# Stick-breaking heads of two pairs begun together: products adjacent, masks after them, the second set inside the next V projection

## The chip, the cores and the metric

The kernel runs on one core of a Trainium2 chip. The metric is the device time of one execution in microseconds (us). The time before is the median of three runs; beside them stands one profiled execution, from which all rows here come.

## What is computed

A decoder trunk of two layers on 256 tokens of width 1024 in float32. Layer 0 runs 8 stick-breaking heads and 4 differential heads on one input projection, then an output projection and an MLP; layer 1 is a sparse attention with its own MLP. The change touches the stick-breaking heads of layer 0 alone:

```python
def stick_breaking_attention(q, k, v):
    ...
        z = jnp.einsum("bqhd,bkhd->bhqk", qb, k).astype(jnp.float32) * scale
        log_beta = jax.nn.log_sigmoid(z)
        log_rem = jnp.where(past, jax.nn.log_sigmoid(-z), 0.0)
        tail = lax.cumsum(log_rem, axis=3, reverse=True) - log_rem
        w = jnp.where(past, jnp.exp(log_beta + tail), 0.0)
        return jnp.einsum("bhqk,bkhd->bqhd", w.astype(v.dtype), v)
```

The heads are 64 wide, and `past` is strict: a query sees only earlier keys.

## The kernel before

Activations stay in SBUF, in two token tiles of 128 and transposed in eight slices of 128 features. Each weight arrives by DMA in two halves (`Weights.load`, L48), is split into a high part by ScalarE (`wh`, L66) and a low part by VectorE (`wl`, L69), and is kept in four rotating buffers; `get` (L78) splits one weight ahead in the program's order. A projection is three products per slice: high by high, high by low, low by high. A product of float32 operands (scores, values) appears as two records in the trace.

The work is written with a tile framework. Python order gives each instruction its priority; the framework then orders every engine's queue, and it may place an instruction that is ready ahead of an earlier one that is not. It also puts in all waits. Each engine works its queue in the order so made.

Layer 0's mixer (`even_mixer`, L487) goes in this order: V of the stick-breaking heads (`project_v`, L492: 24 products of 512 columns for token tile 0 into one PSUM bank, a copy by ScalarE, then 24 for tile 1 into another); the first halves of Q and K (`halves`, L511: `ps_f` products, copied to `qsb` and `ksb` by ScalarE at L509); the first set, `sb_start` for pairs 0 and 1 (L520); the second halves of Q and K; `sb_weights` for pairs 0 and 1; the second set, `sb_start` for pairs 2 and 3 (L523); `scalars` (L163: five small loads, one tiny product `ps_lam` and a few small operations for lambda); V of the differential heads, `project_v("dfv")`; `sb_values` of pairs 0 and 1 (`osb`); `sb_weights` of pairs 2 and 3; then the differential heads' projections and scores (`sdf`).

A pair is two heads, which lie on the lower and upper 64 partitions of `q` and `k`. `sb_start` (L552) takes a score tile `z` of two PSUM banks, one for each head. There are two such tiles, so pairs 2 and 3 use those of pairs 0 and 1 again. For each head it issues two products on 64 rows (256 columns, then 128) and two masks, products of the 128 x 128 identity with the mask in bfloat16 on all 128 rows. Then comes the softplus of the pair: three steps on ScalarE (`sb_e`, L569 to L571: absolute value, exponential, logarithm), and on VectorE `sb_sp` (L572), its high part `sb_h` (L573) and its low part `sb_l` (L574). `sb_weights` (L577) adds the suffix sums to `z` by products on `sb_h`, then `sb_l`, and ScalarE writes `sb_w` as the exponential (L586), the last reader of `z`.

Of the kernel before, what the change touches and what calls it, by code (L numbers as in the profile page):

```python
# [10 lines left out]
F32 = mybir.dt.float32  # L11
# [7 lines left out]
P = 128  # L19
S = 256  # L20
# [65 lines left out]
class Trunk:  # L86
# [400 lines left out]
    def even_mixer(self, xT, oT, pool, out):  # L487
        nc = self.nc
        vsb = pool.tile([P, 2, 512], F32, name="vsb")
        vdf = pool.tile([P, 2, 512], F32, name="vdf")  # L490

        def project_v(key, dst):  # L492
            w = [self.W.get((key, 0)), None]
            pss = [self.bankB("ps_v0"), self.bankB("ps_v1")]
            self.tmajor(pss[0], w[0], xT, 0, range(4), True, False)
            w[1] = self.W.get((key, 1))
            self.tmajor(pss[0], w[1], xT, 0, range(4, 8), False, True)
            nc.scalar.copy(dst[:, 0, :], pss[0])
            self.run_late()
            self.tmajor(pss[1], w[0], xT, 1, range(4), True, False)  # L500
            self.tmajor(pss[1], w[1], xT, 1, range(4, 8), False, True)
            nc.scalar.copy(dst[:, 1, :], pss[1])

        def project_f(key, i, dst, scale):
            w = self.W.get((key, i))
            for m in range(2):
                ps = self.bankB("ps_f")
                self.fmajor(ps[:, :S], w, m, xT)
                nc.scalar.activation(dst[:, 2 * i + m, :], ps[:, :S], AF.Copy, scale=scale)  # L509

        def halves(i, a, b, q, k):  # L511
            project_f(a, i, q, 0.125)
            project_f(b, i, k, 1.0)

        qsb = pool.tile([P, 4, S], F32, tag="q", name="qsb")
        ksb = pool.tile([P, 4, S], F32, tag="k", name="ksb")
        project_v("sbv", vsb)
        halves(0, "sbq", "sbk", qsb, ksb)
        with self.tc.tile_pool(name="ps_sb", bufs=2, space=PSUM) as banks:
            sb = {pr: self.sb_start(pr, qsb, ksb, pool, banks) for pr in (0, 1)}  # L520
            halves(1, "sbq", "sbk", qsb, ksb)
            w = {pr: self.sb_weights(sb[pr], pool) for pr in (0, 1)}
            sb = {pr: self.sb_start(pr, qsb, ksb, pool, banks) for pr in (2, 3)}  # L523
            self.scalars()
            project_v("dfv", vdf)
            for pr in (0, 1):
                self.sb_values(pr, w[pr], vsb, oT)
            w = {pr: self.sb_weights(sb[pr], pool) for pr in (2, 3)}
        qdf = pool.tile([P, 4, S], F32, tag="q", name="qdf")
        kdf = pool.tile([P, 4, S], F32, tag="k", name="kdf")  # L530
        halves(0, "dfq", "dfk", qdf, kdf)
        for pr in (2, 3):
            self.sb_values(pr, w[pr], vsb, oT)
        with self.tc.tile_pool(name="ps_df", bufs=4, space=PSUM) as banks:
            a = {h: self.df_weights(h, qdf, kdf, pool, banks) for h in (0, 1)}
            halves(1, "dfq", "dfk", qdf, kdf)
            o = {h: self.df_values(h, a[h], vdf, pool) for h in (0, 1)}
            a = {h: self.df_weights(h, qdf, kdf, pool, banks) for h in (2, 3)}
            for h in (0, 1):
                self.df_norm(h, o[h], oT, pool)  # L540

            def rest0():
                for h in (2, 3):
                    o[h] = self.df_values(h, a[h], vdf, pool)

            def rest1():
                for h in (2, 3):
                    self.df_norm(h, o[h], oT, pool)

            return out(banks, (rest0, rest1))  # L550

    def sb_start(self, pr, q, k, pool, banks):  # L552


        nc = self.nc
        z = banks.tile([P, 1024], F32, tag="z", name=f"z{pr}").rearrange("p (h c) -> p h c", h=2)
        N = S + P
        for h in range(2):
            d = slice(64 * h, 64 * h + 64)
            self.mm(z[:, h, :S], k[d, pr, :P], q[d, pr, :], True, False, skip_group_check=True)  # L560
            self.mm(z[:, h, S:N], k[d, pr, P:], q[d, pr, P:], False, False, skip_group_check=True)
            for c in (0, S):
                self.mm(z[:, h, c : c + P], self.identb, self.maskb, False, False, skip_group_check=True)
        zv = z[:, :, :N]
        e = pool.tile([P, 2, N], F32, tag="sb_e", name="sb_e", bufs=2)
        sp = pool.tile([P, 2, N], F32, tag="sb_sp", name="sb_sp", bufs=2)
        sph = pool.tile([P, 2, N], F32R, tag="sb_h", name="sb_h", bufs=2)
        spl = pool.tile([P, 2, N], F32R, tag="sb_l", name="sb_l", bufs=2)
        nc.scalar.activation(e, zv, AF.Abs)  # L569
        nc.scalar.activation(e, e, AF.Exp, scale=-1.0)  # L570
        nc.scalar.activation(e, e, AF.Ln, bias=1.0)  # L571
        nc.vector.scalar_tensor_tensor(sp, zv, 0.0, e, op0=ALU.max, op1=ALU.add)  # L572
        nc.vector.tensor_copy(sph, sp)  # L573
        nc.vector.tensor_sub(spl, sp, sph.bitcast(F32))  # L574
        return z, sph, spl
# [584 lines left out]
```

## Time and profile before

| what | value |
|---|---|
| median of three runs | 667.12 us |
| lowest run | 666.63 us |
| the profiled execution | 669.41 us |
| its span, first to last instruction | 667.7 us |
| mean granted TensorE clock | 0.985 |

The profile's engines are PE (TensorE's products), PEld (its weight loads), DVE (VectorE), ACT (ScalarE), POOL (GpSimd) and SP, which issues the loads. A record has its start from the beginning of the span and its length; records of products overlap, as the engine is pipelined. "Idle before" is the time for which the engine had stood, with the instruction that ended it. The granted clock is the share of 2.4 GHz that TensorE had.

### The profile page before, as it was taken

To read this page: it belongs to the slowest core of one execution; us is meant where nothing else is said; L and a number is where in the kernel's file an instruction comes from. 1 tells how busy PE (TensorE), PEld (TensorE's weight loads), DVE (VectorE), ACT (ScalarE), POOL (GpSimd) and SP (SyncE) were. 2 spreads that over 40 slices of the span, in tenths; PEclk is the share of its full clock that TensorE was granted. 3 is DMA by queue.
4 is the path that set the end of the run, shared out by engine and by line. 5 is a ranking of instruction groups with operands and counts; after the bars stand their busy time and mean duration, and the time that the engine had idled before them with its cause. 6 is when DMAs were issued, how large, how long until landed. Compare 5 with 4: busy or idle time off the path is not lost.

```text
span 667.7 us, 11136 instructions
## 1 busy us (share of the span) xinstructions
PE 647.5 (97%) x4257; PEld 566.6 (85%) x4257; DVE 408.4 (61%) x820; ACT 346.7 (52%) x699; POOL 46.3 (7%) x139
## 2 busy tenths in 40 slices
PE   6899999999999999999999989999999999999995
PEld 3798898889989898988898878777899899998984
DVE  5854637886555555555877485776775555555534
ACT  5565556555444444444567464753554445454423
POOL 3200000000000000000203321430000000000000
PEclk7999899999999999999999999999999999999998
DMA  7784243346555555555597632023365555656601
GB/s 255 229 261 138 71 149 127 116 156 212 188 183 189 182 182 183 184 186 143 155 319 243 194 110 64 1 64 124 110 222 180 188 188 190 189 190 185 192 2 63
DMA packets 74277, 108.67 MB, mean 163 GB/s; under 512 B 5072, under 2 KB 60400, under 8 KB 74224
## 3 DMA queue, kind: packets, MB, share of 16 engines
q1 hardware_dynamic: 74224, 107.97, 50.6%
q8 instruction: 33, 0.54, 0.3%
q14 instruction: 20, 0.16, 0.1%
HBM read 106.91 MB, written 1.05 MB: 162 GB/s over the span
## 4 chain that ended last, share of the span: by engine, by line
PE 90%; DVE 5%; ACT 2%; issue 1%; DMA 1%; SPq 0%; ACTq 0%; DVEq 0%
PE macc L108 26%; PE ps_up L108 24%; PE ps_f L108 7%; PE acc L108 4%; PE ps_q L108 4%; PE ps_ut L108 3%; PE ps_v L108 3%; PE o L108 2%; PE s L108 2%; PE z L108 2%; PE ps_or L108 2%; PE ps_k L108 2%; PE pt L1015 2%; DVE wl L69 1%; PE ps_h L108 1%
## 5 line engine op out<-in xcount | busy, mean ns | idle before, releaser
L69 DVE TENSOR_TENSOR wl<-w,wh 128x1024 fp32r<-128x1024 f32 (+1 forms) x188 | 225.1, 1214 | 176.8 <-ACT wh L66 176.5
L66 ACT CAST wh<-w 128x1024 fp32r<-128x1024 f32 (+1 forms) x190 | 192.9, 1040 | 176.0 <-PE macc L108 83.3
L108 PE MATMUL macc<-wh,l 128*128 128x512 f32 x256 | 101.2, 395 | 0.0
L108 PE MATMUL macc<-wh,h 128*128 128x512 f32 x256 | 101.1, 395 | 0.0
L108 PE MATMUL macc<-wl,h 128*128 128x512 f32 x256 | 101.0, 394 | 0.0
L108 PE MATMUL ps_up<-m0h,wh 128*128 128x256 f32 x224 | 63.4, 283 | 0.0
L108 PE MATMUL ps_up<-m1h,wh 128*128 128x256 f32 x224 | 63.4, 283 | 0.0
L108 PE MATMUL ps_up<-m0h,wl 128*128 128x256 f32 x224 | 63.3, 283 | 0.0
L108 PE MATMUL ps_up<-m1h,wl 128*128 128x256 f32 x224 | 63.3, 283 | 0.0
L108 PE MATMUL ps_up<-m1l,wh 128*128 128x256 f32 x224 | 63.3, 283 | 0.0
L108 PE MATMUL ps_up<-m0l,wh 128*128 128x256 f32 x224 | 63.3, 283 | 0.0
L108 PEld LDWEIGHTS macc<-wh,l 128*128 128x128 f32 x256 | 48.2, 188 | 11.2
L108 PEld LDWEIGHTS macc<-wh,h 128*128 128x128 f32 x256 | 48.4, 189 | 10.0
L108 PEld LDWEIGHTS macc<-wl,h 128*128 128x128 f32 x256 | 48.3, 188 | 10.0
L108 PEld LDWEIGHTS ps_up<-m0l,wh 128*128 128x128 f32 x224 | 42.9, 191 | 0.6
L108 PEld LDWEIGHTS ps_up<-m1l,wh 128*128 128x128 f32 x224 | 42.8, 191 | 0.6
L108 PEld LDWEIGHTS ps_up<-m0h,wh 128*128 128x128 f32 x224 | 42.8, 191 | 0.6
L108 PEld LDWEIGHTS ps_up<-m1h,wh 128*128 128x128 f32 x224 | 42.8, 191 | 0.6
L108 PEld LDWEIGHTS ps_up<-m1h,wl 128*128 128x128 f32 x224 | 42.9, 191 | 0.0
L108 PEld LDWEIGHTS ps_up<-m0h,wl 128*128 128x128 f32 x224 | 42.9, 191 | 0.0
L972 POOL TENSOR_SCALAR p<-p,sums 128x128 f32<-128x128 f32 (+1 forms) x64 | 31.4, 508 | 80.5 <-ACT kd L709 25.9
L108 PE MATMUL ps_f<-x0h,wh 128*128 128x256 f32 x128 | 36.4, 285 | 0.0
(285 smaller groups left out, 1202.9 us busy)
## 6 DMA issues: line engine op xcount, KB each, us to landing
w<-in_mlp_w_dram SPq DMA_DIRECT2D x128, 512.0 KB, 4.3
w<-in_ev_w_in_dram SPq DMA_DIRECT2D x24, 512.0 KB, 4.9
w<-in_od_w_in_dram SPq DMA_DIRECT2D x18, 512.0 KB, 5.3
w<-in_ev_w_out_dram SPq DMA_DIRECT2D x8, 512.0 KB, 4.3
w<-in_od_w_out_dram SPq DMA_DIRECT2D x8, 512.0 KB, 3.6
cwk<-in_od_cmp_k_w_dram SPq DMA_DIRECT2D x8, 256.0 KB, 6.0
cwv<-in_od_cmp_v_w_dram SPq DMA_DIRECT2D x8, 256.0 KB, 5.7
w<-in_od_w_in_dram SPq DMA_DIRECT2D x4, 304.0 KB, 3.0
```

The costliest lines, as they stand in the source:

```text
L66: self.nc.scalar.copy(wh[:, c], w)
L69: eng.tensor_sub(wl[:, c], w, wh[:, c].bitcast(F32))
L108: self.nc.tensor.matmul(out, lhsT, rhs, start=start, stop=stop, **kw)
L972: nc.gpsimd.tensor_scalar(o[:, h], o[:, h], sums[:, h : h + 1], 0.0, op0=ALU.mult, op1=ALU.add)
L1015: nc.tensor.transpose(pt[:, h * P : (h + 1) * P], p[g, t, b][:, h, kt * P : (kt + 1) * P], self.ident)
```

## The change

`sb_start` takes a list of pairs. It first takes the score tiles of all of them and issues the products: for each pair, the 256-column product of head 0, of head 1, then the 128-column product of head 0, of head 1. Behind the products of both pairs come all masks, eight in a row. Then the softplus of each pair, now a function of its own, unchanged. The number and sizes of all instructions stay.

The second set moves. `project_v` takes a function `between`, called after the first token tile's copy; the set for pairs 2 and 3 is begun there, between token tiles 0 and 1 of the differential heads' V, and so also behind `scalars`.

```diff
-        def project_v(key, dst):
+        def project_v(key, dst, between=None):
...
             self.run_late()
+            if between is not None:
+                between()
             self.tmajor(pss[1], w[0], xT, 1, range(4), True, False)
...
-            sb = {pr: self.sb_start(pr, qsb, ksb, pool, banks) for pr in (0, 1)}
+            sb = self.sb_start((0, 1), qsb, ksb, pool, banks)
             halves(1, "sbq", "sbk", qsb, ksb)
             w = {pr: self.sb_weights(sb[pr], pool) for pr in (0, 1)}
-            sb = {pr: self.sb_start(pr, qsb, ksb, pool, banks) for pr in (2, 3)}
             self.scalars()
-            project_v("dfv", vdf)
+            sb = {}
+            project_v("dfv", vdf, lambda: sb.update(self.sb_start((2, 3), qsb, ksb, pool, banks)))
...
-    def sb_start(self, pr, q, k, pool, banks):
...
-        z = banks.tile([P, 1024], F32, tag="z", name=f"z{pr}").rearrange("p (h c) -> p h c", h=2)
+    def sb_start(self, prs, q, k, pool, banks):
         N = S + P
-        for h in range(2):
-            d = slice(64 * h, 64 * h + 64)
-            self.mm(z[:, h, :S], k[d, pr, :P], q[d, pr, :], True, False, skip_group_check=True)
-            self.mm(z[:, h, S:N], k[d, pr, P:], q[d, pr, P:], False, False, skip_group_check=True)
-            for c in (0, S):
-                self.mm(z[:, h, c : c + P], self.identb, self.maskb, False, False, skip_group_check=True)
+        zs = [banks.tile([P, 1024], F32, tag="z", name=f"z{pr}").rearrange("p (h c) -> p h c", h=2) for pr in prs]
+        for pr, z in zip(prs, zs):
+            for kt, c in ((0, slice(0, S)), (1, slice(S, N))):
+                for h in range(2):
+                    d = slice(64 * h, 64 * h + 64)
+                    self.mm(z[:, h, c], k[d, pr, kt * P : (kt + 1) * P], q[d, pr, kt * P :], kt == 0, False,
+                            skip_group_check=True)
+        for z in zs:
+            for h in range(2):
+                for c in (0, S):
+                    self.mm(z[:, h, c : c + P], self.identb, self.maskb, False, False, skip_group_check=True)
+        return {pr: self.sb_softplus(z, pool) for pr, z in zip(prs, zs)}
+
+    def sb_softplus(self, z, pool):
...
```

## Rows read from the trace of the kernel before

**Rows 1.** The page: TensorE's share, its clock in 40 slices, the last chain.

```profile
PE 647.5 (97%) x4257; PEld 566.6 (85%) x4257; DVE 408.4 (61%) x820; ACT 346.7 (52%) x699; POOL 46.3 (7%) x139
...
PEclk7999899999999999999999999999999999999998
...
PE 90%; DVE 5%; ACT 2%; issue 1%; DMA 1%; SPq 0%; ACTq 0%; DVEq 0%
```

**Rows 2.** The chain in order of time, 40 to 86 us: start, length, what.

```profile
42.02 4.26 PE z L108 x24
...
60.02 0.71 ACT sb_w L586
...
60.78 5.43 PE z L108 x24
66.21 0.52 PE ps_lam L108 x2
66.73 12.85 PE ps_v L108 x48
```

**Rows 3.** Busy time by stretches; the first line names the columns.

```profile
core 0: us, PE busy (x) PEld busy (x) DVE busy (x) ACT busy (x) POOL busy (x), PEclk, DMA share, GB/s
41.95:46.09 4.14, 4.14 (x26) 3.11 (x25) 1.22 (x1) 3.89 (x5) 0.00 (x0) 1.00 0.95 325
...
60.08:63.54 3.46, 2.76 (x15) 2.14 (x16) 1.20 (x1) 1.87 (x3) 0.00 (x0) 1.00 0.66 188
63.54:70.37 6.83, 6.83 (x22) 5.02 (x21) 2.55 (x6) 4.28 (x7) 0.00 (x0) 0.50 0.18 61
```

**Rows 4.** PE's timeline, first set: start, length, operation, count [idle before].

```profile
41.95 0.92 PE L108 MATMUL z<-qsb,ksb 64*128 64x256 f32 x4
42.80 0.29 PE L108 MATMUL z<-maskb,identb 128*128 128x128 bf16 x2
43.02 0.92 PE L108 MATMUL z<-qsb,ksb 64*128 64x256 f32 x4
...
46.09 0.36 PE L108 MATMUL ps_f<-x0h,wh 128*128 128x256 f32 x1
```

**Rows 5.** The tile z: length of one mask in ns, least, median, most.

```profile
L108 PE MATMUL z<-maskb,identb x16: 219/229/314, 42.8 to 65.9; 128*128 128x128 bf16 x16
```

**Rows 6.** PE's timeline: second set's start, V projection, the last `sb_weights`' low part.

```profile
60.78 0.92 PE L108 MATMUL z<-qsb,ksb 64*128 64x256 f32 x4 [0.71 <-ACT sb_w L586]
...
72.16 1.07 PE L108 MATMUL ps_v<-wh,x0l 128*128 128x512 f32 x4
73.07 1.07 PE L108 MATMUL ps_v<-wl,x0h 128*128 128x512 f32 x4
...
82.78 0.39 PE L108 MATMUL z<-sb_l,negU 128*128 128x384 f32 x1
```

**Rows 7.** ACT's timeline as the first set begins.

```profile
41.94 1.04 ACT L66 CAST wh<-w 128x1024 fp32r<-128x1024 f32 x1 [2.38 <-PE ps_f L108]
42.89 0.38 ACT L509 ACTIVATE ksb<-ps_f 128x256 f32<-128x256 f32 x1
```

**Rows 8.** PE's timeline, scores of two differential heads and what follows.

```profile
96.51 1.69 PE L108 MATMUL sdf<-kdf,qdf 64*128 64x128 f32 x16
98.13 0.38 PE L108 MATMUL ps_f<-x0h,wh 128*128 128x256 f32 x1
```

**Rows 9.** ACT's timeline, end of the second softplus and the next casts.

```profile
68.42 0.16 ACT L180 ACTIVATE lam_e<-ps_lam 128x2 f32<-128x2 f32 x1
68.56 0.84 ACT L571 ACTIVATE sb_e<-sb_e 128x768 f32<-128x768 f32 x1
...
75.99 2.01 ACT L66 CAST wh<-w 128x1024 fp32r<-128x1024 f32 x2 [1.23 <-PE ps_v L108]
```

**Rows 10.** DVE's timeline, the last low part and the next subtractions.

```profile
71.76 0.96 DVE L574 TENSOR_TENSOR sb_l<-sb_sp,sb_h 128x768 fp32r<-128x768 f32 x1
...
77.08 2.36 DVE L69 TENSOR_TENSOR wl<-w,wh 128x1024 fp32r<-128x1024 f32 x2 [4.36 <-ACT wh L66]
```

More of the change, by code (lines that the diff above doesn't have):

```diff
@@ L550, in even_mixer @@
             return out(banks, (rest0, rest1))
-    def sb_start(self, pr, q, k, pool, banks):
+    def sb_start(self, prs, q, k, pool, banks):
+        N = S + P
+        zs = [banks.tile([P, 1024], F32, tag="z", name=f"z{pr}").rearrange("p (h c) -> p h c", h=2) for pr in prs]
[11 more added lines that the diff above has]
+    def sb_softplus(self, z, pool):
         nc = self.nc
-        z = banks.tile([P, 1024], F32, tag="z", name=f"z{pr}").rearrange("p (h c) -> p h c", h=2)
         N = S + P
-        for h in range(2):
-            d = slice(64 * h, 64 * h + 64)
-            self.mm(z[:, h, :S], k[d, pr, :P], q[d, pr, :], True, False, skip_group_check=True)
-            self.mm(z[:, h, S:N], k[d, pr, P:], q[d, pr, P:], False, False, skip_group_check=True)
-            for c in (0, S):
-                self.mm(z[:, h, c : c + P], self.identb, self.maskb, False, False, skip_group_check=True)
         zv = z[:, :, :N]
```

## The prediction
> **What bounds the kernel now.** I read the page's shares first, then the chain of waits through the stretch that the change touches, then the granted clock by stretches, then the engines' timelines there. TensorE is busy 97% of the span and the chain that ended last runs through it for 90% [rows 1]: what the change saves on TensorE's queue counts in full, unless something later waits for it, and what it saves elsewhere counts nothing. In the chain [rows 2] the reader should see that the second set of stick-breaking scores costs 5.43 us after 0.71 us spent on `sb_w`, the exponential of pair 0, and that the V projection behind it takes 12.85 us. The windows [rows 3] tell why these pieces are long: the clock stood at 1.00 up to 63.54 us and at 0.50, the 1.2 GHz level, for the 6.83 us up to 70.37. The slices of [rows 1] show no such stretch again before the last slice.
>
> **Why the clock fell there.** Before it, TensorE was busy 2.76 of 3.46 us (60.08 to 63.54), with products on 64 of the 128 rows after the idle 0.71 us [rows 3, 6]. The first set is the same work without the pause, 4.14 us at a clock of 1.00 with none lost behind it [rows 3]. So the pause and the long run of half-array products together brought the clock down, as far as these rows tell. At half clock 6.83 us of work need 3.42 us at full clock: 3.41 us lost. By pieces of the chain: the second set, 5.43 us against 4.26 for the first, gives 1.2; the scalar product's 0.52 gives 0.26 [rows 2]; the V projection has 12 groups of four matmuls that start 0.91 us apart at full clock [rows 6], 10.9 us against 12.85, which gives 1.95. That sums to 3.4 too.
>
> **Part 1: the products of two heads adjacent, masks behind all of them.** Before, each head runs its products from 41.95 to 42.80, 0.85 us, and its two masks to 43.02, 0.22 us; four heads fill 4.14 us up to 46.09 [rows 4]. The masks use all 128 rows, so the heads run one behind the other. What two heads cost when nothing stands between them is shown by `sdf`, the differential heads' scores: the same count and sizes of products (8, half of 128 and half of 256 columns, 64 rows, two row halves, two banks) go from 96.51 to the next operation's start at 98.13, 1.62 us, switching included [rows 8], where four times 0.85 would be 3.4. The stick-breaking heads of a pair lie in two banks as well (512 columns each). Eight masks behind one another: two take 0.22 with the switch back [rows 4], and two together last 0.29 where one lasts 0.22 at least [rows 4, 5], so each further one adds about 0.07: 0.22 + 6 x 0.07 = 0.64. A packed set is 1.62 + 0.64 = 2.26 us, 1.9 less than 4.14. The other end of this price is no concurrency: 3.4 + 0.64 = 4.04, a gain of 0.1. I take 1.9, since `sdf` is the same form on the same engine.
>
> **The first set has a wait of its own.** Pair 1 needs `ksb` of the second half. ScalarE casts a weight from 41.94 and copies that `ksb` at 42.89 for 0.38 us, done at 43.27 [rows 7]; today pair 1 starts two heads of 1.07 us after 41.95, at 44.1, and never sees it. Now pair 0 is through its products at about 42.75 and pair 1 stands until 43.3. From there 0.85 us of products and 0.64 of masks: about 44.8 against 46.09, a gain of 1.3. The ends are 1.9, if the instruction order fills the hole, and 1.0. Queued behind the waiting products on TensorE are the masks and the next `ps_f`; their readers wait with them, but pair 0's softplus begins at 44.2 today and `sb_weights` follows only after 11.5 us of `ps_f`, so nobody feels it.
>
> **Part 2: the second set between the token tiles.** The set's score tiles reuse the banks of pairs 0 and 1, and today wait 0.71 us for `sb_w` [rows 6]. In the new place 24 V matmuls (5.45 us by the 0.91 pace) stand between, and `sb_w`, of which the chain has 0.71 us [rows 2], ends in their shadow. The gain is 0.71, and packing 1.9. With no pause before it, the set is 2.3 us of denser work amid full-array matmuls, half as long as the first set that kept its clock. I take the clock as kept: 3.4. Second set together: 6.0.
>
> **What is late next.** `sb_weights` of pairs 2 and 3 needs the softplus of that set. Today the whole V projection covers it: scores done at 66.21, last `sb_l` done at 71.76 + 0.96 = 72.72, needed 82.78 [rows 2, 6, 10]. Only the second token tile covers it now. Count from the end of the first `sb_weights`, 0: scalar product 0.35 (estimate from 0.52 at half clock plus a switch), first tile to 5.8, scores to 8.1, second tile to 13.5. The last `sb_l` is needed 82.78 - 79.58 = 3.2 us after the V projection (the chain's 66.73 + 12.85 = 79.58), at 16.7. ScalarE has six operations of 0.84 us, 5.0 in all; the last ends at 69.40 today, and VectorE's tail behind it is 72.72 - 69.40 = 3.3 us [rows 9, 10]: ready at 8.1 + 0.1 + 5.0 + 3.3 = 16.5. So 0.2 us of slack. What can eat it are the weight casts that today start at 75.99, released halfway through the second tile (now about 10.8, in the middle of the softplus): a small `lam_e` activation already slipped between two softplus steps [rows 9]. One cast is 1.0 us (2.01 for two) and one subtraction on VectorE 1.2 (2.36 for two) [rows 9, 10]: a wait of 0 to 2.0 us. I charge 0.7, below the middle, because the softplus precedes the casts in the program. Behind the waiting `sb_weights` on TensorE stand the next `ps_f`, and for those ScalarE's copies; both only shift.
>
> By the Trainium skill, TensorEngine Tiling (Array Packing), Performance Considerations, PSUM Bottleneck, packing speeds up TensorE but not what empties PSUM, which may then bind. By that rule the wait is at its upper end or at rival B's, and the sum below is 1.3 to 3.5 us smaller; no run so far shows a TensorE wait here.
>
> **What costs nothing.** `scalars` now precedes the second set; its loads are issued by SP in the same order, as scores issue none, and behind its small operations stands nothing new. Weight transfers are paced by buffers that TensorE frees, so they move earlier with it, and they have room: 0.18 of the DMA engines from 63.54 to 70.37 [rows 3]. The later stages keep their lengths.
>
> **Sum.** 1.3 + 6.0 - 0.7 = 6.6 us. The profiled execution took 669.41 us (span 667.7) and would take 662.8; the median of the runs, 667.12, lies 2.3 below it and becomes 660.5.
>
> **Rivals.**
> A, the forecast, 660.5; its own range has the first set at 1.9 and no wait, 659.2, and the first set at 1.0 with a wait of 2.0, 662.1: chance 0.62.
> B, the wait for the softplus is long: two casts and two subtractions ahead, 2.0 + 2.4 - 0.2 = 4.2 us, so 667.12 - 7.3 + 4.2 = 664.0. For it: thin slack. Against: the casts' buffer comes free only when half the softplus is past. 0.14.
> C, the clock falls all the same: first or second set, 3.4 us dearer, 663.9. For it: half-array work and a new hole of 0.5 us in the first set. Against: the first set held its clock over 4.14 us. 0.12. The Trainium skill, TensorE: Matmul & The Clock Gate, Why this matters for your kernels, blames idle gaps between bursts, and longer ones than this kernel has here; by it the 0.71 us alone would not have sufficed, so taking it away would not keep the clock, and C would hold. The trace has a fall behind 0.71 us, so gap and products count together.
> D, the change doesn't do what it says: heads do not overlap. Each set gains 0.1 instead of 1.9 (the first loses no time to `ksb` then), so 0.1 + 0.71 + 3.4 + 0.1 - 0.7 = 3.6: 663.5. Against it stands `sdf`. 0.06.
> E, slower: the softplus is queued behind all four casts and subtractions of the V weights, 4 x 1.0 + 4 x 1.2 - 0.2 = 8.6 us of wait, more than the 7.3 gained: 668.4, and 671.8 if the clock falls in that hole. It decides from a wait of 7.3 us. Against: two of these casts need the second V weight's buffer, free only at the end of the second tile, when ScalarE's part of the softplus is over. 0.06.
>
> A to D hold 0.94 and lie between 659.2 and 664.0; I widen by about one below and above, for terms sized a little wrong and the spread of executions: 658.0 to 665.0, leaving out E and the edges of B and C, some 0.2. A measurement of this kernel tells changes of about 2%, 13.3 us, from none: faster than 653.8 would need twice the gain, 0.02; slower than 680.5 needs E twice over, 0.03; same 0.95.
>
> **What would show it.** Right: the first set about 2.9 us long with a hole near its middle, ended by `ksb`; the second about 2.3 us, no idle before it; a clock of 1.00 through both V tiles; the V projection's 24-matmul halves 5.45 us each; a TensorE wait of at most 2 us before or within the last `sb_weights`, ended by VectorE's `sb_l` or `sb_h`. Wrong: score products one behind the other in time, a stretch at 0.50 near 45 to 75 us, a long idle time before the last `sb_weights`, or other projections pulled in between, which would hide that wait and save 0.7 more.

## The result and the profile after

| | changed kernel | kernel before | ratio, 95% interval |
|---|---|---|---|
| first comparison, medians | 663.02 us (six runs) | 668.2 us (six runs) | 0.9919 [0.99, 0.9939] |
| second comparison, medians | 661.85 us (six runs) | 668.09 us (18 runs) | 0.9906 [0.9881, 0.993] |
| profiled execution (span) | 662.43 us (660.7) | 669.41 us (667.7) | |
| mean granted TensorE clock of it | 0.991 | 0.985 | |

The kernel is 5.4 us faster by the first comparison (4.1 to 6.7, from the interval), less than 2%. The forecast was 660.5 us within 658.0 to 665.0: sign and range held, and the time was 2.5 us too hopeful. One of the six runs of the kernel before took 1045.58 us, far above all others, and the ratio is that of the fast runs alone. The profiled execution of the kernel before, 669.41 us, lies in the upper part of that kernel's runs, a point that comes back below.

The chain of waits of the changed kernel from 40 to 77 us, in order of time (start, length, what); its lines answer [rows 2]:

```profile
42.55 1.04 ACT wh L66
43.59 0.29 ACT ksb L511
43.88 0.04 issue
43.92 1.48 PE z L108 x16
45.40 11.57 PE ps_f L108 x96
56.97 2.24 PE z L108 x16
59.21 0.31 PE ps_lam L108 x2
59.52 5.66 PE ps_v L108 x24
65.19 2.06 PE z L108 x24
67.25 5.50 PE ps_v L108 x24
72.75 1.50 PE osb L108 x16
74.25 2.44 PE z L108 x16
```

The 0.71 us for `sb_w` are gone. The second set, 5.43 us in [rows 2], is 2.06 us long and lies between two V tiles of 5.66 and 5.50 us, which were 12.85 us together. Behind the second V tile the last `sb_weights` follows `osb` with no wait. What has come in is a short wait in the first set: ScalarE's cast and then `ksb`.

TensorE's timeline of the changed kernel at both sets (start, length, operation, count, idle before); it answers [rows 4, 6]:

```profile
42.55 0.92 PE L108 MATMUL z<-qsb,ksb 64*128 64x256 f32 x8
43.92 0.92 PE L108 MATMUL z<-qsb,ksb 64*128 64x256 f32 x8 [0.45 <-ACT ksb L511]
44.78 0.62 PE L108 MATMUL z<-maskb,identb 128*128 128x128 bf16 x8
45.21 0.37 PE L108 MATMUL ps_f<-x0h,wh 128*128 128x256 f32 x1
...
65.12 1.58 PE L108 MATMUL z<-qsb,ksb 64*128 64x256 f32 x16
66.63 0.62 PE L108 MATMUL z<-maskb,identb 128*128 128x128 bf16 x8
67.06 1.16 PE L108 MATMUL ps_v<-wh,x0h 128*128 128x512 f32 x4
```

By starts, the first set takes 45.21 - 42.55 = 2.66 us and the second 67.06 - 65.12 = 1.94, where the old order took 4.14 at full clock. The eight records of a pair's two heads now run side by side: 0.92 us for both heads, as long as one head took alone in [rows 4].

Busy time by stretches, columns as in [rows 3]: from the first set's start to the first `ps_f` of the differential heads, and from there to the end. I call the first stretch the region; all versions below are compared by its length. First the changed kernel, then the kernel before:

```profile
42.55:76.52 33.97, 33.52 (x243) 29.98 (x243) 17.77 (x25) 23.34 (x35) 0.00 (x0) 1.00 0.41 132
76.52:660.73 584.21, 572.41 (x3844) 505.35 (x3842) 362.29 (x759) 299.35 (x629) 37.22 (x113) 1.00 0.50 161
```

```profile
41.95:83.36 41.41, 40.70 (x244) 34.82 (x243) 22.59 (x28) 24.85 (x35) 0.00 (x0) 0.92 0.45 140
83.36:667.67 584.31, 572.50 (x3844) 505.24 (x3842) 358.22 (x755) 298.98 (x628) 37.23 (x113) 1.00 0.50 159
```

All that this pair of executions differs by lies in the region: 41.41 - 33.97 = 7.44 us. The rest of the program is the same within 0.1 us. The region began 0.60 us later in the changed kernel, ahead of any instruction that the change touches; over the traces of this case, with and without the change, it begins anywhere between 40.67 and 43.55. So 7.44 - 0.60 + 0.10 = 6.94 us of span.

### The profile page after: what moved, and what is told of

It is laid out like the page before. It is cut to its first block, busy times and chain, and to the rows that moved or that the text cites. A ratio compares the mean times of both kernels' runs of the same rounds, so it can differ in the third digit from the quotient of the medians.

```text
span 660.7 us, 11136 instructions
## 1 busy us (share of the span) xinstructions
PE 641.3 (97%) x4257; PEld 562.2 (85%) x4257; DVE 407.7 (62%) x820; ACT 345.5 (52%) x699; POOL 46.3 (7%) x139
## 3 DMA queue, kind: packets, MB, share of 16 engines
HBM read 106.91 MB, written 1.05 MB: 163 GB/s over the span
## 4 chain that ended last, share of the span: by engine, by line
PE 90%; DVE 5%; ACT 2%; issue 1%; DMA 1%; SPq 0%; ACTq 0%; DVEq 0%
PE macc L108 27%; PE ps_up L108 24%; PE ps_f L108 7%; PE acc L108 5%; PE ps_q L108 4%; PE ps_ut L108 3%; PE ps_v L108 2%; PE o L108 2%; PE s L108 2%; PE ps_or L108 2%; PE ps_k L108 2%; PE pt L1026 2%; DVE wl L69 2%; PE z L108 1%; PE ps_h L108 1%
```

## The experiments

The questions: what is each part worth by itself; was it the pause or the half-array products that brought the clock down before, and how much does that cost on average; what does the adjacency of the two heads add to taking the masks out from between; and why did the softplus not hold up the last `sb_weights`. Each diff is against the changed kernel unless it says otherwise.

### The changed kernel again

> The changed kernel once more, beside the runs of the kernel before on this chip. My account: between the first set's start and the first ps_f of the differential heads the changed kernel needs 33.97 us where the kernel before needs 41.41, 7.4 less, and the rest of the span is equal, so a ratio of 0.989. Rival (something behind the stretch gives part of it back in most executions): a ratio of 0.992 or more again, with a second stretch at half clock or new idle time of TensorE behind 77 us in the trace.

Measured: 661.85 us (661.02 to 663.42) against 668.09, ratio 0.9906 [0.9881, 0.993]. That lies between the 0.989 expected and the rival's 0.992, and the interval holds both. The region has 33.97 us again, to the hundredth. But this execution has a stretch at half clock elsewhere, in layer 1. Its windows, columns as before, the region, the rest and that stretch:

```profile
41.98:75.95 33.97, 33.52 (x243) 29.96 (x243) 17.67 (x25) 23.34 (x35) 0.00 (x0) 1.00 0.44 140
75.95:661.71 585.76, 573.96 (x3844) 506.57 (x3842) 362.05 (x759) 299.46 (x629) 37.23 (x113) 0.99 0.51 160
...
378.00:381.40 3.40, 3.40 (x18) 3.40 (x17) 2.50 (x9) 1.16 (x5) 0.00 (x0) 0.50 0.17 59
```

The rest is 585.76 - 584.21 = 1.55 us longer than in the first trace. Just before, TensorE works through small products and waits 0.79 us for an activation (`fsv`) ahead of `ps_q`; the first trace has the same 0.79 us at the same place and kept its clock. So the change is not needed for it: one trace of four of the kernel before has it too (at 381.60), and four of the ten with a change. These are too few to tell whether the change makes it more frequent.

### Packing alone

```diff
             w = {pr: self.sb_weights(sb[pr], pool) for pr in (0, 1)}
+            sb = self.sb_start((2, 3), qsb, ksb, pool, banks)
             self.scalars()
-            sb = {}
-            project_v("dfv", vdf, lambda: sb.update(self.sb_start((2, 3), qsb, ksb, pool, banks)))
+            project_v("dfv", vdf)
```

The second set stands at its old place, so the pause is kept; both sets are packed. It was profiled in two executions.

> Both sets packed, the second set left at its old place, ahead of scalars and the V projection. Theory 1 (the clock fell before because a pause of 0.71 us and a long run of half-array products came together): the pause stays, the set is 2.1 us, the clock stays at 1.00; slower than the changed kernel by the pause alone, 0.7 us, ratio 0.990. Theory 2 (the pause alone brings the clock down): a stretch at 0.50 again, 3.4 us lost, ratio 0.995. Theory 3 (unpacked half-array products alone did it): as theory 1.

> Both sets packed, the second left behind its pause, a second trace. If the pause and a long set of half-array products are both needed for the fall of the clock: none between 60 and 75 us again, and 34.75 us from the first set to the differential heads' ps_f. If the pause alone can do it in some executions: a stretch at 0.50 there and 36.4 us or more.

Measured: 663.69 us (662.36 to 665.7) against 668.09, ratio 0.993 [0.9904, 0.9955]; the second execution took 663.08. The ratio lies between the 0.990 of the first theory and the 0.995 of the second and does not decide; the traces do. TensorE's timeline at the second set, then the two executions' regions:

```profile
60.75 1.62 PE L108 MATMUL z<-qsb,ksb 64*128 64x256 f32 x16 [0.71 <-ACT sb_w L597]
```

```profile
43.39:78.14 34.75, 33.59 (x243) 30.12 (x243) 21.99 (x28) 24.23 (x35) 0.00 (x0) 1.00 0.49 154
```

```profile
42.38:77.14 34.76, 33.60 (x244) 30.13 (x243) 21.99 (x28) 24.24 (x35) 0.00 (x0) 1.00 0.52 161
```

The pause is there in full, 0.71 us, and the clock stays at 1.00 in both. The region is 0.78 us longer than the changed kernel's: in these two traces the move is worth little more than the pause once the sets are packed. By the medians packing alone is 1.84 us behind the changed kernel; the two intervals overlap, and a fall of the clock in executions that were not traced is not excluded.

### The move alone

```diff
         for pr, z in zip(prs, zs):
-            for kt, c in ((0, slice(0, S)), (1, slice(S, N))):
-                for h in range(2):
-                    d = slice(64 * h, 64 * h + 64)
+            for h in range(2):
+                d = slice(64 * h, 64 * h + 64)
+                for kt, c in ((0, slice(0, S)), (1, slice(S, N))):
                     self.mm(z[:, h, c], k[d, pr, kt * P : (kt + 1) * P], q[d, pr, kt * P :], kt == 0, False,
                             skip_group_check=True)
-        for z in zs:
-            for h in range(2):
                 for c in (0, S):
                     self.mm(z[:, h, c : c + P], self.identb, self.maskb, False, False, skip_group_check=True)
```

> The second set moved between the token tiles, both sets in the old order, head by head with masks between. No pause ahead of the second set. Theory 1 (pause and products together): clock 1.00 throughout, sets of 4.1 us each, gain over the kernel before 0.7 + 3.4 = 4.1 us, ratio 0.994. Theory 2 (pause alone): the same. Theory 3 (half-array products alone bring the clock down): a stretch at 0.50 behind the second set, gain 0.7 us, ratio 0.999.

Measured: 665.99 us (median of 12, 665.1 to 668.38) against 668.09, ratio 0.9975 [0.9957, 0.9993]. The 0.994 of the first theory, which counts 3.4 us for the clock, lies outside the interval, and the 0.999 of the third lies inside; the trace decides. Its region:

```profile
42.28:79.95 37.67, 37.67 (x243) 32.65 (x243) 20.18 (x27) 24.65 (x35) 0.00 (x0) 1.00 0.40 126
```

TensorE is busy without a break, the clock is kept, and the two sets have their old 4.14 us each. So the third theory is out for this execution. The ratio fell short because the fall of the clock costs less on average than 3.4 us: with the 1.9 us worked out below, the gain is 0.71 + 1.9 = 2.6 us, a ratio of 0.996, inside the interval. Against the changed kernel that is 37.67 - 33.97 = 3.70 us, which is what packing saves: 4.14 - 2.66 = 1.48 in the first set and 4.14 - 1.94 = 2.20 in the second. Eleven of its 12 runs lie within 1.3 us (665.1 to 666.35), where the kernel before spreads over 5.6 us (665.39 to 671.01). Much of what varied from run to run seems to have gone with the move. That is not a proof by itself: the seven runs of packing alone spread over 3.3 us, with no fall in either trace.

### The kernel before, three more traces

No edit.

> The kernel before, unchanged, for a second trace. If the fall of the clock behind the pause is the same in every execution: 6.83 us at 0.50 near 64 us again and 41.4 us from the first set to the differential heads' ps_f. If its length varies from execution to execution: 3.4 us at 0.50 or none, and 38 to 39.7 us, which would be why the median of the runs gained less than the traced pair of executions.

> The kernel before, a third trace. The first had the clock at 0.50 for 6.83 us behind the pause and 41.41 us from the first set to the differential heads' ps_f; the second had no fall there and 38.35. If the fall varies from execution to execution: 41.4, 39.7 or 38.4 us, according to the length of a stretch at 0.50 between 60 and 75 us. If the second trace was an exception: 41.4 again.

> The kernel before, a fourth trace, for the same question: 38.35 us from the first set to the differential heads' ps_f without a fall of the clock, 41.4 with one of 6.83 us, about 39.7 with one of half that length.

Measured: 667.52, 669.45 and 668.41 us, one execution each. The region, and where there is one, the stretch at half clock behind the pause, in that order:

```profile
41.77:80.12 38.35, 37.64 (x243) 32.74 (x243) 22.42 (x28) 24.86 (x35) 0.00 (x0) 1.00 0.51 156
```

```profile
43.55:83.50 39.95, 39.24 (x244) 33.89 (x243) 22.59 (x28) 24.85 (x35) 0.00 (x0) 0.96 0.43 135
...
67.10:70.50 3.40, 3.40 (x9) 2.62 (x10) 2.18 (x5) 2.79 (x5) 0.00 (x0) 0.50 0.01 3
```

```profile
41.00:82.43 41.43, 40.72 (x244) 34.81 (x243) 22.59 (x28) 24.85 (x35) 0.00 (x0) 0.92 0.43 133
...
62.10:68.90 6.80, 6.80 (x20) 5.01 (x21) 1.54 (x4) 4.74 (x7) 0.00 (x0) 0.50 0.28 81
```

The same program, with the same pause, lost nothing there in the first (which has the stretch in layer 1 instead), 39.95 - 38.35 = 1.60 us in the second and 41.43 - 38.35 = 3.08 in the third; the trace of the prediction lost 41.41 - 38.35 = 3.06. Mean over the four: 1.9 us. The 18 runs of the second comparison fit this, though a mean clock does not say where it fell: five lie at 665.4 to 665.9 us with a mean clock of 0.990 or 0.991, the others at 667.3 to 671.0, most of these at 0.983 to 0.989.

### Half-array products twice, without a pause

```diff
-                for kt, c in ((0, slice(0, S)), (1, slice(S, N))):
+                for kt, c in 2 * ((0, slice(0, S)), (1, slice(S, N))):
```

This diff is against the move alone. Every score product is issued twice, so this kernel does extra work: 1.50 us of half-array products a head between the masks where the kernel before has 0.85, and no pause.

> Both sets in the old order and the second one moved (no pause ahead of it), with every score product issued twice, the first result overwritten: extra work on purpose, 2.6 us more of half-array products in each set, each set 6.7 us long. If half-array products alone bring the clock down, given enough of them: a stretch at 0.50 behind one of the two sets. If the pause is needed: clock 1.00 from the first set to the differential heads' ps_f, and 37.67 + 5.2 = 42.9 us for this stretch.

Measured: 669.65 us (one execution), region:

```profile
40.67:83.58 42.91, 42.91 (x275) 37.42 (x275) 21.89 (x28) 25.36 (x35) 0.00 (x0) 1.00 0.40 126
```

A head with its masks now takes 1.72 us instead of 1.07, and the clock stays at 1.00. So the half-array products alone did not bring it down here, nor did the pause alone (packing alone, two traces); before, with both, it came down in three traces of four.

### Masks last, heads not adjacent

```diff
         for pr, z in zip(prs, zs):
-            for kt, c in ((0, slice(0, S)), (1, slice(S, N))):
-                for h in range(2):
-                    d = slice(64 * h, 64 * h + 64)
+            for h in range(2):
+                d = slice(64 * h, 64 * h + 64)
+                for kt, c in ((0, slice(0, S)), (1, slice(S, N))):
```

> The changed kernel with the products of a pair head by head (256 and 128 columns of head 0, then of head 1), masks still behind all of them. If taking the masks away from between the heads is what packs them, as in the differential heads' scores, which are written in this order: the second set again 2.0 to 2.3 us, no difference to the changed kernel. If adjacency of two heads' equal products is needed: products one behind the other, each set 1.3 us longer, ratio to before 0.993.

Measured: 663.19 us against 668.09, ratio 0.992 [0.9895, 0.9945]. TensorE's timeline at the second set:

```profile
64.45 1.68 PE L108 MATMUL z<-qsb,ksb 64*128 64x256 f32 x16
66.06 0.62 PE L108 MATMUL z<-maskb,identb 128*128 128x128 bf16 x8
```

All four heads' products take 66.06 - 64.45 = 1.61 us, against 66.63 - 65.12 = 1.51 with the heads adjacent; one behind the other they would need four times 0.85. In the records the first products of the two heads start 14 ns apart, although both of head 0's products stand ahead of head 1's in TensorE's queue. (The two records of one head's product start 0.32 us apart in the kernel before, so these are two heads.) So TensorE itself began the other row half's product early; that it works its queue strictly in order, as is said of each engine ahead of the prediction, does not hold here. Taking the masks out from between is what packs the heads. Their adjacency adds 0.1 us in the second set, 1.94 instead of 2.04; the first set has 2.66 us in both versions.

The Trainium skill, TensorEngine Tiling (Array Packing), Key Properties, says that a change of tiling mode drains TensorE. The traces agree: a mask on all 128 rows between the heads keeps them 1.07 us apart, and without it they run together. The Trainium skill, TensorE: Matmul & The Clock Gate, The mechanism, says that products start strictly in queue order and only weight loads are pulled ahead. The start 14 ns behind, across a product that was queued in between, differs from that; the measurement decides.

### Masks after each pair

```diff
                     self.mm(z[:, h, c], k[d, pr, kt * P : (kt + 1) * P], q[d, pr, kt * P :], kt == 0, False,
                             skip_group_check=True)
-        for z in zs:
             for h in range(2):
                 for c in (0, S):
```

Pair 0's masks stand ahead of pair 1's products, so they can fill the wait for `ksb`, at the price of one more switch in each set.

> The changed kernel with each pair's four masks straight behind that pair's products. First set: the masks of pair 0 fall into the hole in which TensorE waits for ksb (0.45 us), so they are free there and the set is about 0.2 us shorter, 2.45 instead of 2.66. Second set: one more switch between 64-row products and 128-row masks, and pair 1 cannot run ahead under pair 0's tail: 0.2 us longer, 2.1 to 2.2 instead of 1.94. Net nothing. If the hole is not the wait for ksb but something of TensorE's own, the first set gets longer too.

Measured: 662.31 us (one execution), region 34.47, that is 0.50 more than the changed kernel. TensorE's timeline at the first set and in the last `sb_weights`, then one line of ScalarE's and four of VectorE's:

```profile
41.89 0.92 PE L108 MATMUL z<-qsb,ksb 64*128 64x256 f32 x8
42.74 0.40 PE L108 MATMUL z<-maskb,identb 128*128 128x128 bf16 x4
43.26 0.92 PE L108 MATMUL z<-qsb,ksb 64*128 64x256 f32 x8
44.12 0.40 PE L108 MATMUL z<-maskb,identb 128*128 128x128 bf16 x4
...
75.74 0.44 PE L108 MATMUL z<-sb_l,negU 128*128 128x384 f32 x1 [0.17 <-DVE sb_l L584]
```

```profile
69.27 1.05 ACT L66 CAST wh<-w 128x1024 fp32r<-128x1024 f32 x1
...
72.00 1.22 DVE L69 TENSOR_TENSOR wl<-w,wh 128x1024 fp32r<-128x1024 f32 x1
73.13 0.55 DVE L583 CAST sb_h<-sb_sp 128x768 fp32r<-128x768 f32 x1
73.60 1.22 DVE L69 TENSOR_TENSOR wl<-w,wh 128x1024 fp32r<-128x1024 f32 x1
74.73 0.95 DVE L584 TENSOR_TENSOR sb_l<-sb_sp,sb_h 128x768 fp32r<-128x768 f32 x1
```

The first set gains 0.23 us (2.43 instead of 2.66), the second loses 0.31 (2.25 instead of 1.94), as expected. What was not expected is a third item: the last `sb_weights` takes 2.73 us instead of 2.34 and now waits for `sb_l`. The 0.31 us of the second set alone would not have used up the softplus's slack, which is 0.6 us in the changed kernel. What did it is what the prediction feared: in this version's order a weight cast on ScalarE (1.05 us) and two subtractions on VectorE (1.22 us each) stand between the last pair's softplus steps.

### `ksb` on VectorE

```diff
         def halves(i, a, b, q, k):
             project_f(a, i, q, 0.125)
-            project_f(b, i, k, 1.0)
+            project_f(b, i, k, 1.0, nc.vector if b == "sbk" else None)
```

With an engine given, `project_f` copies `ps_f` by that engine's `tensor_copy`. So `ksb` of the stick-breaking heads no longer stands behind ScalarE's weight cast.

> The changed kernel with the copies of K for the stick-breaking heads on VectorE, which is idle there, instead of ScalarE, where a weight cast of 1.04 us stands ahead of the last of them. If that cast is what pair 1 waits for, the hole of 0.45 us in the first set is gone or under 0.15 us, and the span shorter by that; in the ratio (about 0.0006) it cannot be told apart from the changed kernel, 0.991. If the hole stays, it was not the cast.

Measured: 661.5 us (661.05 to 662.14) against 668.23, ratio 0.9892 [0.9859, 0.9924]. TensorE's timeline at the first set, then the region:

```profile
42.90 1.60 PE L108 MATMUL z<-qsb,ksb 64*128 64x256 f32 x16
44.44 0.62 PE L108 MATMUL z<-maskb,identb 128*128 128x128 bf16 x8
44.87 0.36 PE L108 MATMUL ps_f<-x0h,wh 128*128 128x256 f32 x1
```

```profile
42.90:76.17 33.27, 33.27 (x244) 29.95 (x243) 18.88 (x28) 22.41 (x32) 0.00 (x0) 1.00 0.42 131
```

The hole is gone: the first set is 44.87 - 42.90 = 1.97 us, close to the second set's 1.94, and TensorE is busy all through the region, which is 0.70 us shorter. This is the best version here by its region; its median is too near the changed kernel's for the runs to tell them apart.

### The second set later still

```diff
             self.run_late()
+            self.tmajor(pss[1], w[0], xT, 1, range(4), True, False)
             if between is not None:
                 between()
-            self.tmajor(pss[1], w[0], xT, 1, range(4), True, False)
```

The set begins when half of tile 1's V products are through, so the softplus has 2.7 us less cover.

> The changed kernel with the second set begun behind the first half of token tile 1's V products, 2.7 us later. My account of the slack (the softplus is done 0.6 us ahead of its last use in the changed kernel): the last sb_weights wait about 2 us for sb_h and sb_l, and the stretch from the first set to the differential heads' ps_f is 36 us instead of 33.97. Rival (slack is ample, or other projections are pulled ahead): no idle time there and 34.0 us.

Measured: 663.55 us (one execution). Up to the `ps_f` behind the last `sb_weights` it is 36.20 us, as expected, but not for the reason expected: other work stands in that stretch. So the stretch from the first set to the second `osb` is the one to compare: 45.94 us, against 45.63 of the changed kernel. The chain of waits in order of time:

```profile
72.08 1.50 PE osb L108 x16
73.58 2.11 PE ps_f L108 x16
75.69 2.56 PE z L108 x16
```

The wait of about 2 us that I expected is not there. The framework had put 16 of the next projection's products, 2.11 us, ahead of `sb_weights`, since those were ready and the softplus was not. The work had to be done anyway, so the late set cost 0.3 us. This was the fourth case under "what would show it", the projections pulled in between.

## Why the prediction was right, and where its size was off

**What bounds the kernel now.** Right. What the change took off TensorE's queue came off the span one for one: 7.44 us of the region, 0.10 of the rest, less the 0.60 by which the region began later.

**The terms of the sum**, predicted, measured in this pair of executions, and on average:

| term | predicted | this pair | on average |
|---|---|---|---|
| first set | 1.3 | 1.48 | 1.48 |
| packing of the second set | 1.9 | 2.20 | 2.20 |
| pause for `sb_w` | 0.71 | 0.71 | 0.71 |
| clock | 3.4 | 3.06 | 1.9 |
| wait for the softplus | -0.7 | 0 | 0 |
| sum | 6.6 | 7.4 | 6.3 |

The averages are the regions': the four traces of before have 40.29 us in the mean, the changed kernel 33.97 in both of its traces. Without a stretch at half clock the difference is 38.35 - 33.97 = 4.38 us, and 1.48 + 2.20 + 0.71 is 4.39. That the forecast 6.6 comes so near the 6.3 is in part luck: the clock was put 1.5 us too high, and the other terms together 1.2 us too low.

**Packing.** Right, from the right row. `sdf` [rows 8] gave 1.62 us for four heads' worth of products; they took 1.51, and eight masks 0.43 where I had worked out 0.64.

**The first set's own wait.** Right: a hole in its middle, ended by `ksb`, of 0.45 us where about half a microsecond was worked out. Putting `ksb` on VectorE removed it, so the cause is shown.

**The clock: the mis-sized term.** The mechanism held: the clock of the changed kernel is 1.00 through the region, and of the pause and the half-array products neither alone brought it down. (Each "alone" rests on two traces; with before losing nothing in one of four, two such traces could come by chance once in 16. The 12 runs of the move alone, which spread far less, speak for it as well.) The size failed: 3.4 us were read from one execution, and it was one of the costly ones. On average over the four traces the fall took 1.9 us.

**The sum's last step: where the miss comes from.** Of the 2.5 us between 660.5 and 663.02, 1.1 is the base: the median of three, 667.12, had the run of 1045.58 us in it and so rested on two ordinary runs; six runs have 668.2. The other 1.4 is the gain, 5.2 us between the medians instead of 6.6. I had shifted the profiled 669.41 to 667.12 and taken the whole 6.6 off it. But the runs of before differ in part by this very fall: by their mean clock, the five at 665.4 to 665.9 seem to have had none. (Not by it alone: the region's start varies by 2.9 us over the traces.) A median that lies 2.3 us below the profiled execution has probably lost part of the 3.4 already, and I took it off a second time. Without the shift the sum gives 669.41 - 6.6 = 662.8; the profiled execution of the changed kernel took 662.43. By averages it is 668.1 - 6.3 = 661.8; the second comparison has 661.85. The first has 663.02, above rival A's own range (up to 662.1), for which the stretch at half clock in layer 1, 1.55 us in some executions of both kernels, is the candidate. "The later stages keep their lengths" held between the two first traces and does not hold for every execution.

**What is late next.** The account was close: counted from the end of the first `sb_weights` at 59.21, the scores ended at 8.04 (8.1 predicted), the last `sb_l` was needed at 16.7 (16.7). The changed kernel's ScalarE, VectorE and TensorE lines, in this order:

```profile
69.99 1.58 ACT L582 ACTIVATE sb_e<-sb_e 128x768 f32<-128x768 f32 x2
71.46 1.99 ACT L66 CAST wh<-w 128x1024 fp32r<-128x1024 f32 x2
```

```profile
73.54 1.82 DVE L585 TENSOR_TENSOR sb_l<-sb_sp,sb_h 128x768 fp32r<-128x768 f32 x2
```

```profile
75.95 0.39 PE L108 MATMUL z<-sb_l,negU 128*128 128x384 f32 x1
```

The casts that I feared came behind the softplus's last step, the last `sb_l` was done at 75.36, and 0.6 us of slack were left. So the 0.7 us charged were not paid. The fear was sound all the same: with the masks after each pair, one cast and two subtractions did come between the softplus steps, and TensorE waited 0.17 us.

**The rivals.** B, the long wait for the softplus: no, the changed kernel has none, and where the cover was shortened the order filled it with other products. C, the clock falls all the same: not in the region of any of the ten traces with a change. D, the heads do not overlap: they do; the move alone shows how long the sets are when they do not, 4.14 us where D supposed 4.04. E, slower: no. On rival C's page, the Trainium skill, TensorE: Matmul & The Clock Gate, Why this matters for your kernels, blames idle gaps longer than this pause. The traces agree in so far as the pause of 0.71 us ahead of a packed set did nothing in two traces; but the clock of the kernel before fell behind just that pause in three of four, so a short one amid half-array products can be enough.

**What stays open.** Why the same program falls behind the pause in one execution and not in the next, and for 3.4 us or 6.8, is not settled by these traces. The same holds for the stretch in layer 1.

## What to carry to other kernels

Keep products on all rows out from between products on row halves: gather the small ones, then the rest, and look at the queue of the engine for what stands between. Price a fall of the clock from several traces, and do not take a loss that varies from run to run off a median that lies below the execution in which you saw it. When a step is moved under shorter cover, work out the slack of what is late next and name what the order could put there instead; here the slack was 0.2 us by the account and 0.6 us on the chip.

## What the runs showed of the hardware that was not expected

TensorE started the product of the other row half 14 ns after the first, past another product in its queue, so the order of the two heads matters little (2.04 against 1.94 us in the second set); full-row masks between the heads matter much: with them a set takes 4.14 us. The stretch at half clock is not a property of the program: four executions of one kernel had 6.83, 0, 3.40 and 6.80 us of it behind the same pause.
